# A diffusion transformer layer: weights split into two fp32r parts, kept in DRAM by the first token block

## The chip, the cores and the metric

The kernel runs on one core of a Trainium2 chip. The metric is the device time of one execution in microseconds (us). The core has engines that run side by side, each through its own list of instructions in order: PE (TensorE, matrix products; its weight loads are listed as PEld), DVE (VectorE), ACT (ScalarE), POOL (GpSimd) and SP, which here only issues transfers. ACT and POOL issue transfers too. All transfers run on the core's 16 DMA engines.

## The reference, cut to what matters

The layer works on 2048 latent tokens of width 1024 (four blocks of 512) and 256 context tokens.

```
n = modulate(rmsnorm(x))                                # the context tokens alike
q, k, v, u, gate_attn, gate_ssm = split(n @ w_in)       # 1024 x 4096
att = neighbourhood_attention(rope(q), rope(k), v)      # 8 heads, window 8 x 16 and all context keys
ssm = s5_scans(u); val, gate = split(gelu(ssm) @ w_glu); ssm = val * sigmoid(gate)
mix = (sigmoid(gate_attn) * (att @ w_branch_attn) + sigmoid(gate_ssm) * (ssm @ w_branch_ssm)) @ w_out
h = x + g1 * mix
a, b = split(modulate(rmsnorm(h)) @ w_ffn_in)           # 1024 x 5632
out = rmsnorm(h + g2 * ((silu(a) * b) @ w_ffn_out))
```

## The kernel before, in words

Every product of fp32 matrices is made of three products of fp32r parts (`mm3`, lines 89 to 94): high by high, high by low, low by high. So each weight piece, 128 partitions by 1024 fp32, is loaded (`raw`, line 73), its high part is a copy to fp32r on ACT (line 70) and its low part the difference on DVE (line 71). `piece` (line 79) does the three steps. The raw pieces have two buffers (`wr`; three in the merges, four in the FFN), the parts three each (`wh`; four in the FFN).

`cols` (line 96) gives products with weights at rest: a piece feeds one or two output column groups over the 512 tokens of a block. `rows` (line 111) gives products with tokens at rest: a column of 256 outputs needs two pieces, of four k-tiles each, and both for every 128 tokens.

The stages, in the order of time:

- `norm_u` norms all tokens, keeps them in DRAM (`ns`) and makes u.
- `in_proj` (line 350) goes over the four token blocks, 28 pieces a block: k, v, q, then the gates. Block 0 has the context tokens too. At the start of block 1 stands `biases`, which makes the attention's bias tables on POOL.
- `s5` and `attention` run at the same time as `in_proj`. A scheduler orders every engine's list by its own estimate of times and by priority: s5 and attention go first, and in-projection and merge work fills TensorE between them.
- `merge` (line 939), once per token block, has 20 pieces: GLU (4, w_glu), the branches (4 of w_bs, 4 of w_ba, in turn), output projection (8, w_out). Its first two blocks run beside attention. `modulation2` loads its own weights there, one piece for each piece of the merge (the generator `between`).
- `ffn` (line 1104) goes over the four blocks: `ffn_in` (line 1026) makes sums of its weights on POOL and seven products in place of eight, then the silu and the second product.

Weights are the same in all token blocks, and each block loads and splits them again. Silu is made as tanh(a/2) on ACT and (1 + t) * a on DVE (lines 1133, 1134); the factor 1/2 that is then missing is in the gate `g[1]` (line 228).

SP issues nearly all transfers: raw weights, q and k stores, s5's small strips (`mt`), attention results (`as`), gates (`gsc`), x. POOL issues the loads of s5's inputs (`ut`, line 651), of the bias tables and of attention (`k`, `kc`, `qh`, `ql`, `vt`, `bi`).

Of the kernel before, what the change touches and what calls it, by code (L numbers as in the profile page):

```python
# [10 lines left out]
F32 = mybir.dt.float32  # L11
# [7 lines left out]
P = 128  # L19
# [33 lines left out]
class Kernel:  # L53
# [24 lines left out]

    def piece(self, src, r, c, nr):

        raw = self.raw(src, r, c, nr)
        with self.hot():
            hi = self.wh.tile([P, nr, 1024 // nr], F32R, name="whi")
            lo = self.wh.tile([P, nr, 1024 // nr], F32R, name="wlo")
            self.split(hi, lo, raw)
        next(self.between, None)
        return hi, lo

# [6 lines left out]

    def cols(self, pool, src, kt, c0, n, ops, tag="ps"):

        nm = 8 // kt  # L100
        for c in range(n):
            w = self.piece(src, 0, c0 + c, kt)
            for m in range(nm):
                sl = slice(m * P, (m + 1) * P)
                for i, (nt, f) in enumerate(ops):
                    ps = pool.tile([P, nt], F32, name=tag)
                    for k in range(kt):
                        self.mm3(ps, (w[0][:, k, sl], w[1][:, k, sl]), f(k), k == 0, k == kt - 1)
                    yield c * nm + m, i, ps

    def rows(self, pool, src, c, ops, tag="ps"):


        w = [self.piece(src, r, c, 4) for r in range(2)]
        for i in range(0, len(ops), 2):
            ps = pool.tile([P, 2, 256], F32, name=tag)
            for j in range(2):
                for k in range(KD):
                    self.mm3(ps[:, j], ops[i + j](k), (w[k // 4][0][:, k % 4], w[k // 4][1][:, k % 4]), k == 0, k == KD - 1)
            yield i, ps  # L120
# [6 lines left out]
    def constants(self):  # L127
# [21 lines left out]
        self.us = d.tile([LA, AW], F32, name="us")  # L149
        self.ns = d.tile([NB, KD, P, 2, TB], F32, name="ns")  # L150
        self.gsc = d.tile([2, KD, NB, P, TB], F32, name="gsc")
        self.hs = d.tile([L, D], F32, name="hs")
# [55 lines left out]
    def modulation2(self, tp, pp):  # L208
# [4 lines left out]
        for sec in (2, 3, 4, 5):  # L213
            for c2 in range(2):
# [9 lines left out]
                if sec in (2, 5):  # L224
                    pg = pp.tile([P, 512], F32, name="ps")
                    nc.tensor.matmul(pg, self.ones, acc, start=True, stop=True)
                    with self.hot():
                        V.tensor_scalar(self.g[sec // 5][:, c2 * 512:c2 * 512 + 512], pg, 0.5, None, op0=ALU.mult)
                else:
# [120 lines left out]
    def in_proj(self, ring, ev, pm, nt, nct):  # L350
        nc, I = self.nc, self.I
        V = nc.vector
        for b in range(NB):
            if b:
                nt = [ring.tile([P, 2, TB], F32R, name="n") for _ in range(KD)]
                for k in range(KD):
                    nc.sync.dma_start(nt[k].bitcast(F32), self.ns[b, k])
            t0 = b * TB
            cs = ev.tile([P, 2, TB], F32, name="cs", bufs=1)
            nc.sync.dma_start(cs, I["rope"][:, :, t0:t0 + TB])  # L360
# [9 lines left out]
            def qk(c0, ops, isk):  # L370
                for jj, i, ps in self.cols(pm, I["w_qk"], KD, c0, 4, ops):
                    with self.hot():
# [31 lines left out]
            for c in range(2):  # L404
# [3 lines left out]
                oc = slice(c * 256, c * 256 + 256)  # L408
                for i, ps in self.rows(pm, I["w_vu"], c, ops):
                    e = ev.tile([P, 2, 256], F32, name="e")  # L410
# [11 lines left out]
            for gi in range(2):  # L422
                for m, _, ps in self.cols(pm, I["w_gate"], KD, gi * 8, 8, [lat]):
                    g = ev.tile([P, TB], F32, name="e")
                    with self.hot():
                        nc.scalar.activation(g, ps, AF.Tanh, scale=0.5)
                    nc.scalar.dma_start(self.gsc[gi, m, b], g)
# [511 lines left out]
    def merge(self, b, yp, mp, tp, pm):  # L939
# [5 lines left out]
        op = [(TB, lambda k: (y[k][:, 0], y[k][:, 1]))]  # L945
        ssm = []
        for m2 in range(2):
            tg = []
            for _, _, ps in self.cols(pm, I["w_glu"], 4, 2 + m2, 1, op):
                t = tp.tile([P, TB], F32, name="t")  # L950
                with self.hot():
                    nc.scalar.activation(t, ps, AF.Tanh, scale=0.5)
                tg.append(t)
            for m, _, ps in self.cols(pm, I["w_glu"], 4, m2, 1, op):
                s = yp.tile([P, 2, TB], F32R, name="y")
# [11 lines left out]
        for m2 in range(4):  # L967
            part = {}
            for z, wn, gi in ((ssm, "w_bs", 1), (att, "w_ba", 0)):
                for m, _, ps in self.cols(pm, I[wn], 4, m2, 1, [(TB, lambda k, z=z: (z[k][:, 0], z[k][:, 1]))]):  # L970
                    mm = m2 * 2 + m
# [9 lines left out]
        for c in range(4):  # L981
            cs = slice(c * 256, c * 256 + 256)
            ops = [lambda k, j=j: (mh[:, k, j * P:(j + 1) * P], ml[:, k, j * P:(j + 1) * P]) for j in range(4)]
            for i, ps in self.rows(pm, I["w_out"], c, ops):
                ts = slice(b * TB + i * P, b * TB + (i + 2) * P)
# [40 lines left out]
    def ffn_in(self, ch, b, X, pm, os, tp, up):  # L1026
# [33 lines left out]
        for x in src:  # L1060
            with self.hot():
                hi = self.wh.tile([P, x.shape[1], 4, P], F32R, name="whi")
                lo = self.wh.tile([P, x.shape[1], 4, P], F32R, name="wlo")
                self.split(hi.rearrange("p a k m -> p a (k m)"), lo.rearrange("p a k m -> p a (k m)"), x)
# [39 lines left out]
    def ffn(self, xs_, os, xp, tp, pm, first):  # L1104
        nc, I = self.nc, self.I
        V = nc.vector
        with ExitStack() as ctx:
# [13 lines left out]
            for b in range(NB):  # L1121
# [4 lines left out]
                for g, (p0, p1) in enumerate(groups):  # L1126
                    last = g == len(groups) - 1
                    zs = {}
                    for m2 in range(p0, p1):
                        ts = []  # L1130
                        for a in self.ffn_in(m2, b, X, pm, os, wp, up):
                            t = wp.tile([P, TB], F32, name="n")
                            nc.scalar.activation(t, a, AF.Tanh, scale=0.5)
                            V.scalar_tensor_tensor(t, t, 1.0, a, op0=ALU.add, op1=ALU.mult)
                            ts.append(t)
# [218 lines left out]
```

## Time and profile before

| | |
|---|---|
| median of 3 runs | 3211.07 us (3209.65 to 3219.78) |
| the profiled execution's own time | 3210.19 us |
| its span | 3208.4 us |
| TensorE busy | 3088.2 us, 96% |
| DVE / ACT / POOL busy | 2340.6 / 1567.5 / 899.4 us |
| moved by DMA | 564.27 MB, mean 176 GB/s |

The span goes from the first to the last recorded instruction; the time has 1.8 us around it. Busy times of engines overlap, so they do not add up to the span. PE stands for matrix products that are pipelined: an instruction's own duration is longer than its distance to the next. A wait is the idle time of an engine before an instruction, with what ended it.

### The profile page before, as it was taken

How to read it: one execution, taken by the hardware profiler on the slowest of the kernel's cores; microseconds unless marked ns; L12 is line 12 of the kernel's file. 1: busy time of each engine (PE TensorE's matmuls, PEld its weight loads, DVE VectorE, ACT ScalarE, POOL GpSimd, SP SyncE). 2: the span in 40 equal slices, each digit the busy share in tenths (PEclk: the TensorE clock that was granted, in tenths of full speed). 3: DMA queues.
4: the chain of work that ended last, by engine and by line, in shares of the span. 5: the costliest groups of instructions: out<-in, count | busy, mean ns of one | idle time of the engine just before them, and what ended most of it. 6: DMA issues, size and time to landing. Idle time of an engine off the chain costs nothing.

```text
span 3208.4 us, 54284 instructions
## 1 busy us (share of the span) xinstructions
PE 3088.2 (96%) x20600; PEld 2716.4 (85%) x20600; DVE 2340.6 (73%) x4153; ACT 1567.5 (49%) x2746; POOL 899.4 (28%) x856
## 2 busy tenths in 40 slices
PE   7999978999999899999999999999999999999998
PEld 5988766787788788788888998989989998989988
DVE  6689787897753576665657866987868966886766
ACT  4545434454355556466554543454535543554534
POOL 2000053000223232222300544742242423341243
PEclk9999999999999999999999999999999999999999
DMA  8545467454676898887947434434434433443332
GB/s 320 187 126 170 162 195 239 170 163 143 205 242 186 268 277 241 254 250 223 267 152 248 141 122 139 148 129 134 133 128 150 135 112 125 148 145 128 116 109 102
DMA packets 212852, 564.27 MB, mean 176 GB/s; under 512 B 31784, under 2 KB 63656, under 8 KB 212592
## 3 DMA queue, kind: packets, MB, share of 16 engines
q1 hardware_dynamic: 155008, 437.48, 41.4%
q0 software_dynamic: 28032, 87.64, 10.1%
q10 hardware_dynamic: 29552, 35.70, 3.3%
q8 instruction: 162, 2.65, 0.3%
q14 instruction: 98, 0.80, 0.1%
HBM read 446.95 MB, written 111.61 MB: 174 GB/s over the span
## 4 chain that ended last, share of the span: by engine, by line
PE 74%; DVE 10%; DMA 10%; issue 3%; POOL 2%; ACT 1%; SPq 0%; ACTq 0%; POOLq 0%; DVEq 0%
PE ps L92 14%; PE ps L93 14%; PE ps L94 14%; PE ps L1075 8%; PE ps L1073 7%; PE ps L1074 7%; DVE wlo L71 3%; PE o L924 2%; DMA n<-in_rpb 2%; PE w L905 1%; PE w L884 1%; PE pv L750 1%; DMA y<-as 1%; PE c L886 1%; PE c L907 1%
## 5 line engine op out<-in xcount | busy, mean ns | idle before, releaser
L71 DVE TENSOR_TENSOR wlo<-raw,whi 128x1024 fp32r<-128x1024 f32 (+1 forms) x522 | 681.3, 1312 | 338.1 <-ACT whi L70 336.6
L70 ACT CAST whi<-raw 128x1024 fp32r<-128x1024 f32 (+1 forms) x522 | 508.1, 976 | 493.1 <-PE ps L94 184.7
L1073 PE MATMUL ps<-X,whi 128*128 128x256 f32 x2464 | 693.9, 284 | 14.0 <-DVE u L1085 8.6
L1075 PE MATMUL ps<-X,wlo 128*128 128x256 f32 x2464 | 693.3, 284 | 11.6 <-DVE wlo L71 11.5
L1074 PE MATMUL ps<-X,whi 128*128 128x256 f32 x2464 | 690.7, 283 | 0.0
L1073 PEld LDWEIGHTS ps<-X,whi 128*128 128x128 f32 x2464 | 472.0, 192 | 18.3 <-DVE u L1085 11.3
L1075 PEld LDWEIGHTS ps<-X,wlo 128*128 128x128 f32 x2464 | 471.3, 191 | 15.0 <-DVE wlo L71 14.8
L1074 PEld LDWEIGHTS ps<-X,whi 128*128 128x128 f32 x2464 | 472.0, 192 | 0.5
L92 PE MATMUL ps<-n,whi 128*128 128x512 f32 (+1 forms) x800 | 316.8, 396 | 6.9 <-ACT t L382 5.1
L94 PE MATMUL ps<-n,wlo 128*128 128x512 f32 (+1 forms) x800 | 314.8, 394 | 0.0
L93 PE MATMUL ps<-n,whi 128*128 128x512 f32 (+1 forms) x800 | 314.7, 393 | 0.0
L92 PE MATMUL ps<-whi,zh 128*128 128x512 f32 x704 | 277.1, 395 | 0.0
L94 PE MATMUL ps<-whi,zl 128*128 128x512 f32 x704 | 277.0, 394 | 0.0
L93 PE MATMUL ps<-wlo,zh 128*128 128x512 f32 x704 | 276.9, 394 | 0.0
L1056 POOL TENSOR_TENSOR os<-raw 128x512 f32<-128x512 f32 x66 | 117.4, 1779 | 396.7 <-DMA raw<-in_w_f 326.5
L70 ACT CAST whi<-os 128x1024 fp32r<-128x1024 f32 x110 | 115.4, 1049 | 208.7 <-PE ps L1074 83.9
L71 DVE TENSOR_TENSOR wlo<-os,whi 128x1024 fp32r<-128x1024 f32 x110 | 151.7, 1379 | 67.8 <-ACT whi L70 67.8
L92 PEld LDWEIGHTS ps<-n,whi 128*128 128x128 f32 x800 | 150.5, 188 | 46.0 <-ACT t L382 6.8
L93 PEld LDWEIGHTS ps<-n,whi 128*128 128x128 f32 x800 | 150.5, 188 | 34.6 <-issue 3.4
L1057 POOL TENSOR_TENSOR os<-raw,os 128x512 f32<-128x512 f32 x88 | 134.3, 1526 | 161.6 <-DMA raw<-in_w_f 159.7
L94 PEld LDWEIGHTS ps<-n,wlo 128*128 128x128 f32 x800 | 150.4, 188 | 34.1 <-issue 2.0
L92 PE MATMUL ps<-y,whi 128*128 128x512 f32 x384 | 158.4, 414 | 17.0 <-DMA y<-as 9.7
(343 smaller groups left out, 7025.3 us busy)
## 6 DMA issues: line engine op xcount, KB each, us to landing
raw<-in_w_f SPq DMA_DIRECT2D x198, 512.0 KB
raw<-sums SPq DMA_DIRECT2D x66, 512.0 KB
raw<-in_w_gate SPq DMA_DIRECT2D x64, 512.0 KB
raw<-in_w_f SPq DMA_DIRECT2D x66, 256.0 KB
raw<-in_w_qk SPq DMA_DIRECT2D x32, 512.0 KB
gsc<-e ACTq DMA_DIRECT2D x64, 256.0 KB
raw<-in_w_m SPq DMA_DIRECT2D x32, 512.0 KB
t<-gsc SPq DMA_DIRECT2D x64, 256.0 KB
```

The costliest lines, as they stand in the source:

```text
L70: self.nc.scalar.copy(hi, x)
L71: self.nc.vector.tensor_tensor(lo, x, hi.bitcast(F32), op=ALU.subtract)
L92: mm(ps, l[0], r[0], start=first, stop=False)
L93: mm(ps, l[0], r[1], start=False, stop=False)
L94: mm(ps, l[1], r[0], start=False, stop=last)
L750: nc.tensor.matmul(pv[g2 * 64:g2 * 64 + 64, ri, 0:SEQC], win[:, d, p, g2, ri], rhs, start=True, stop=True, skip_group_check=True)
L924: return nc.tensor.matmul(o[h, g, :, hf, :], l, r, start=(n == 0), stop=(n == nb + 1), skip_group_check=True)
L1056: nc.gpsimd.tensor_tensor(s24[:, 0], s13[:, 0], a11, op=ALU.subtract)
L1057: nc.gpsimd.tensor_tensor(s24[:, 1], a12, s24[:, 0], op=ALU.subtract)
L1073: mm(dst, a[0][:, k], xh, start=(first and k == 0), stop=False, skip_group_check=True)
L1074: mm(dst, a[0][:, k], xl, start=False, stop=False, skip_group_check=True)
L1075: mm(dst, a[1][:, k], xh, start=False, stop=(k == 3), skip_group_check=True)
```

## The change

`piece` now has one tile `w` for both parts. In the first token block it loads and splits as before, then stores both parts, 128 x 2048 fp32, to DRAM: from POOL's queue in `in_proj` (tensors `wk`), from SP's in `merge` (tensors `wm`). In the other three blocks it loads both parts by one transfer straight into `w`, with no raw tile and no split. In the FFN nothing is stored; its parts share one tile too. Silu is one activation on ACT, and the factor of `g[1]` is 1.

```diff
-    def piece(self, src, r, c, nr):
-
-        raw = self.raw(src, r, c, nr)
-        with self.hot():
-            hi = self.wh.tile([P, nr, 1024 // nr], F32R, name="whi")
-            lo = self.wh.tile([P, nr, 1024 // nr], F32R, name="wlo")
-            self.split(hi, lo, raw)
+    def piece(self, src, r, c, nr, kept=None, queue=None):
+
+
+        w = self.wh.tile([P, 2, nr, 1024 // nr], F32R, name="w")
+        flat = w.rearrange("p i k f -> p i (k f)").bitcast(F32)
+        if kept is not None and queue is None:
+            self.nc.sync.dma_start(flat, kept)
+        else:
+            raw = self.raw(src, r, c, nr)
+            with self.hot():
+                self.split(w[:, 0], w[:, 1], raw)
+            if kept is not None:
+                queue.dma_start(kept, flat)
         next(self.between, None)
-        return hi, lo
+        return w[:, 0], w[:, 1]
...
+        self.wk = [d.tile([n, P, 2, 1024], F32, name=f"wk{i}") for i, n in enumerate((8, 4, 16))]
+        self.wm = {w: d.tile([n, P, 2, 1024], F32, name=f"wm_{w}") for w, n in (("w_glu", 4), ("w_bs", 4), ("w_ba", 4), ("w_out", 8))}
...
-                        V.tensor_scalar(self.g[sec // 5][:, c2 * 512:c2 * 512 + 512], pg, 0.5, None, op0=ALU.mult)
+                        V.tensor_scalar(self.g[sec // 5][:, c2 * 512:c2 * 512 + 512], pg, 0.5 if sec == 2 else 1.0, None, op0=ALU.mult)
...
+            fill = None if b else nc.gpsimd
...
-                for jj, i, ps in self.cols(pm, I["w_qk"], KD, c0, 4, ops):
+                for jj, i, ps in self.cols(pm, I["w_qk"], KD, c0, 4, ops, kept=self.wk[0], queue=fill):
...
+        fill = None if b else nc.sync
...
-            for i, ps in self.rows(pm, I["w_out"], c, ops):
+            for i, ps in self.rows(pm, I["w_out"], c, ops, kept=self.wm["w_out"], queue=fill):
...
-                hi = self.wh.tile([P, x.shape[1], 4, P], F32R, name="whi")
-                lo = self.wh.tile([P, x.shape[1], 4, P], F32R, name="wlo")
+                hl = self.wh.tile([P, 2, x.shape[1], 4, P], F32R, name="w")
+                hi, lo = hl[:, 0], hl[:, 1]
...
-                            nc.scalar.activation(t, a, AF.Tanh, scale=0.5)
-                            V.scalar_tensor_tensor(t, t, 1.0, a, op0=ALU.add, op1=ALU.mult)
+                            nc.scalar.activation(t, a, AF.Silu)
```

Since the scheduler orders every list anew, instructions move on all engines. POOL's list before, while block 0 of the in-projection runs, holds the loads of s5's inputs (`ut`) and then the first bias load:

```order
L260 TENSOR_TENSOR r<-ms,mhalf 128x4
L651 DMA ut<-us 128x8x64 x2
L651 DMA ut<-us 32x8x64
L651 DMA ut<-us 128x8x64 x2
L651 DMA ut<-us 32x8x64
L651 DMA ut<-us 128x8x64 x2
L651 DMA ut<-us 32x8x64
L651 DMA ut<-us 128x8x64 x2
L651 DMA ut<-us 32x8x64
L651 DMA ut<-us 128x8x64
```

The same place after:

```order
L660 DMA ut<-us 128x8x64
L91 DMA wk_86<-w 128x2048
L660 DMA ut<-us 128x8x64
L660 DMA ut<-us 32x8x64
L91 DMA wk_87<-w 128x2048
L660 DMA ut<-us 128x8x64 x2
L91 DMA wk_87<-w 128x2048
L660 DMA ut<-us 32x8x64
L660 DMA ut<-us 128x8x64
L91 DMA wk_87<-w 128x2048 x2
L91 DMA wk_86<-w 128x2048 x3
L660 DMA ut<-us 128x8x64
```

The stores of the parts (`wk`) stand between the loads.

SP's list before, at the start of merge 0 (`raw` are weights, `in_w_m` those of `modulation2`, `as` attention results out, `y` the branch inputs in, `t<-gsc` gates in):

```order
L936 DMA as<-a 128x1024
L944 DMA y<-ys 128x2x512 x4
L76 DMA raw<-in_w_m 128x1024
L76 DMA raw<-in_w_bs 128x1024
L76 DMA raw<-in_w_m 128x1024
L76 DMA raw<-in_w_ba 128x1024
L76 DMA raw<-in_w_m 128x1024
L973 DMA t<-gsc 128x512 x4
L76 DMA raw<-in_w_bs 128x1024
L973 DMA t<-gsc 128x512
```

The same place after:

```order
L953 DMA y<-ys 128x2x512 x4
L91 DMA wm_w_glu<-w 128x2048
L76 DMA raw<-in_w_m 128x1024
L76 DMA raw<-in_w_bs 128x1024
L76 DMA raw<-in_w_m 128x1024
L91 DMA wm_w_glu<-w 128x2048
L76 DMA raw<-in_w_ba 128x1024
L91 DMA wm_w_bs<-w 128x2048
L76 DMA raw<-in_w_m 128x1024
L945 DMA as<-a 128x1024
L983 DMA t<-gsc 128x512 x4
L91 DMA wm_w_ba<-w 128x2048
```

Each weight piece's store (`wm`) now stands among the loads, behind its split.

SP's list before, at the output projection of merge 3 (`t<-in_x` is x, `in_w_f` the FFN's first weights, `h` its residual):

```order
L76 DMA raw<-in_w_out 128x1024 x2
L973 DMA t<-gsc 128x512 x3
L76 DMA raw<-in_w_out 128x1024
L973 DMA t<-gsc 128x512 x3
L76 DMA raw<-in_w_out 128x1024
L987 DMA t<-in_x 128x2x256
L76 DMA raw<-in_w_out 128x1024
L987 DMA t<-in_x 128x2x256 x2
L1038 DMA raw<-in_w_f 128x1024 x2
L1160 DMA h<-hs 128x512
L987 DMA t<-in_x 128x2x256 x2
L76 DMA raw<-in_w_out 128x1024
```

The same place after:

```order
L85 DMA w<-wm_w_out 128x2048
L983 DMA t<-gsc 128x512
L997 DMA t<-in_x 128x2x256 x2
L85 DMA w<-wm_w_out 128x2048
L997 DMA t<-in_x 128x2x256
L85 DMA w<-wm_w_out 128x2048
L997 DMA t<-in_x 128x2x256
L1048 DMA raw<-in_w_f 128x1024 x3
L997 DMA t<-in_x 128x2x256
L1169 DMA h<-hs 128x512
L997 DMA t<-in_x 128x2x256
L85 DMA w<-wm_w_out 128x2048
```

Loads of both parts stand where raw loads stood; by the list of TensorE each second piece of an output column there is read after 24 products with the first.

## Rows read from the trace of the kernel before

**Rows 1.** The page's busy time of each engine, share of the span and instructions.

```profile
PE 3088.2 (96%) x20600; PEld 2716.4 (85%) x20600; DVE 2340.6 (73%) x4153; ACT 1567.5 (49%) x2746; POOL 899.4 (28%) x856
```

**Rows 2.** Stretches: length, busy us PE, PEld, DVE, ACT, POOL; clock, DMA share, GB/s.

```profile
0.00:160.00 160.00, 141.44 (x1111) 123.60 (x1112) 104.28 (x372) 78.25 (x124) 24.02 (x24) 0.96 0.69 255
160.00:370.00 210.00, 208.65 (x1270) 172.57 (x1270) 169.00 (x360) 100.81 (x219) 10.59 (x13) 1.00 0.50 152
370.00:560.00 190.00, 159.51 (x848) 126.83 (x847) 159.80 (x279) 78.00 (x164) 67.06 (x68) 0.96 0.67 206
560.00:1020.00 460.00, 454.09 (x2578) 367.01 (x2576) 333.30 (x689) 222.18 (x439) 60.88 (x101) 0.99 0.60 186
1020.00:1410.00 390.00, 366.83 (x2539) 309.81 (x2538) 247.34 (x560) 206.83 (x370) 108.17 (x181) 0.97 0.86 257
1410.00:1730.00 320.00, 313.59 (x2272) 273.55 (x2271) 201.58 (x463) 183.77 (x352) 70.42 (x113) 0.99 0.71 220
1730.00:2164.00 434.00, 415.93 (x2924) 387.49 (x2922) 339.58 (x408) 197.19 (x319) 213.98 (x129) 1.00 0.42 144
2164.00:3208.00 1044.00, 1028.14 (x7071) 955.55 (x7071) 785.74 (x1028) 500.43 (x764) 344.24 (x229) 0.99 0.39 128
```

**Rows 3.** Groups by line: shapes, count, busy us, mean ns, idle before and releasers.

```profile
L71 DVE TENSOR_TENSOR wlo<-raw,whi 128x1024 fp32r<-128x1024 f32 x434 | 585.9, 1350 | 319.2 <-ACT whi L70 317.8
...
L70 ACT CAST whi<-raw 128x1024 fp32r<-128x1024 f32 x434 | 454.6, 1048 | 447.4 <-PE ps L94 163.5 <-PE ps L93 104.3 <-PE ps L1074 92.3
...
L1134 DVE SCALAR_TENSOR_TENSOR n<-n 128x512 f32<-128x512 f32 x88 | 65.5, 779 | 0.2
```

**Rows 4.** The page's rate in 40 equal slices of the span.

```profile
GB/s 320 187 126 170 162 195 239 170 163 143 205 242 186 268 277 241 254 250 223 267 152 248 141 122 139 148 129 134 133 128 150 135 112 125 148 145 128 116 109 102
```

**Rows 5.** Waits of TensorE, 400 to 560 us: total us, times, longest.

```profile
PE pv L750 <- DVE p L758: 8.0, 2, 6.4
...
PE ps L92 <- ACT t L382: 3.7, 3, 2.8
...
PE pv L750 <- ACT win L695: 3.0, 1, 3.0
```

**Rows 6.** Groups by line, 370 to 560 us, the split on DVE.

```profile
L71 DVE TENSOR_TENSOR wlo<-raw,whi 128x1024 fp32r<-128x1024 f32 x22 | 28.0, 1273 | 13.2 <-ACT whi L70 13.1
```

**Rows 7.** Waits of TensorE, whole span.

```profile
PE ps L92 <- ACT whi L70: 8.1, 2, 5.2
```

**Rows 8.** Timeline, a column piece of a merge: start us, us; ten products.

```profile
1717.71 0.40 PE L94 MATMUL ps<-y,wlo 128*128 128x512 f32 x1
...
1719.82 0.39 PE L94 MATMUL ps<-y,wlo 128*128 128x512 f32 x1
```

**Rows 9.** Timeline, an output column of a merge: sixteen products.

```profile
1734.85 0.28 PE L94 MATMUL ps<-whi,ml 128*128 128x256 f32 x1
...
1736.61 0.28 PE L94 MATMUL ps<-whi,ml 128*128 128x256 f32 x1
```

**Rows 10.** Chain of waits: start us, us from issue to landing.

```profile
544.93 6.77 DMA ys<-yt
...
667.65 3.20 DMA raw<-in_w_qk
...
1190.72 8.13 DMA raw<-in_w_out
```

**Rows 11.** Waits of TensorE, 1730 to 2200 us.

```profile
PE ps L1073 <- DVE u L1085: 8.0, 9, 1.6
...
PE ps L1075 <- DVE wlo L71: 7.6, 8, 1.7
```

**Rows 12.** Line 171, the table load: ns minimum, median, maximum.

```profile
L171 ACT ACT_TABLE_LOAD  x1: 1283/1283/1283, 2.1 to 2.1; - x1
```

**Rows 13.** Waits of POOL, whole span.

```profile
POOL ut L651 <- ACT un L652: 389.7, 20, 85.5
```

More of the change, by code (lines that the diff above doesn't have):

```diff
@@ L94, in mm3, with cols @@
         mm(ps, l[1], r[0], start=False, stop=last)
-    def cols(self, pool, src, kt, c0, n, ops, tag="ps"):
+    def cols(self, pool, src, kt, c0, n, ops, tag="ps", kept=None, queue=None):
         nm = 8 // kt
         for c in range(n):
-            w = self.piece(src, 0, c0 + c, kt)
+            w = self.piece(src, 0, c0 + c, kt, kept[c0 + c] if kept is not None else None, queue)
             for m in range(nm):
@@ L109, in cols, with rows @@
                     yield c * nm + m, i, ps
-    def rows(self, pool, src, c, ops, tag="ps"):
-        w = [self.piece(src, r, c, 4) for r in range(2)]
+    def rows(self, pool, src, c, ops, tag="ps", kept=None, queue=None):
+        w = [self.piece(src, r, c, 4, kept[c * 2 + r] if kept is not None else None, queue) for r in range(2)]
         for i in range(0, len(ops), 2):
@@ L408, in in_proj @@
                 oc = slice(c * 256, c * 256 + 256)
-                for i, ps in self.rows(pm, I["w_vu"], c, ops):
+                for i, ps in self.rows(pm, I["w_vu"], c, ops, kept=self.wk[1], queue=fill):
                     e = ev.tile([P, 2, 256], F32, name="e")
@@ L422, in in_proj @@
             for gi in range(2):
-                for m, _, ps in self.cols(pm, I["w_gate"], KD, gi * 8, 8, [lat]):
+                for m, _, ps in self.cols(pm, I["w_gate"], KD, gi * 8, 8, [lat], kept=self.wk[2], queue=fill):
                     g = ev.tile([P, TB], F32, name="e")
@@ L946, in merge @@
         ssm = []
+        fill = None if b else nc.sync
         for m2 in range(2):
             tg = []
-            for _, _, ps in self.cols(pm, I["w_glu"], 4, 2 + m2, 1, op):
+            for _, _, ps in self.cols(pm, I["w_glu"], 4, 2 + m2, 1, op, kept=self.wm["w_glu"], queue=fill):
                 t = tp.tile([P, TB], F32, name="t")
@@ L953, in merge @@
                 tg.append(t)
-            for m, _, ps in self.cols(pm, I["w_glu"], 4, m2, 1, op):
+            for m, _, ps in self.cols(pm, I["w_glu"], 4, m2, 1, op, kept=self.wm["w_glu"], queue=fill):
                 s = yp.tile([P, 2, TB], F32R, name="y")
@@ L969, in merge @@
             for z, wn, gi in ((ssm, "w_bs", 1), (att, "w_ba", 0)):
-                for m, _, ps in self.cols(pm, I[wn], 4, m2, 1, [(TB, lambda k, z=z: (z[k][:, 0], z[k][:, 1]))]):
+                for m, _, ps in self.cols(pm, I[wn], 4, m2, 1, [(TB, lambda k, z=z: (z[k][:, 0], z[k][:, 1]))], kept=self.wm[wn], queue=fill):
                     mm = m2 * 2 + m
```

## The prediction

> **What bounds the kernel now.** I read the page's busy times first, then stretches cut at the stages, then what TensorE waited for in each, then the groups by line, the DMA rows and the chain of waits. TensorE is busy 96% of the span [rows 1], and the clock is granted at 0.96 to 1.00 in every stage [rows 2]. What a change off TensorE can win is therefore its idle time, which the stretches split as follows (length less PE busy) [rows 2]: 18.6 us in the norm and u projection, 1.4 in block 0 of the in-projection, 30.5 in block 1 beside the bias tables, 5.9 in blocks 2 and 3, 23.2 in merges 0 and 1 beside attention, 6.4 in merges 2 and 3, 18.1 in the first FFN block and 15.9 in the other three, 120 us in all. The second thing to see there is the DMA column: 0.86 of the 16 engines' time in merges 0 and 1 at 257 GB/s, against 0.42 in the FFN.
>
> **The change part by part.** It removes the split of 28 pieces in each of three in-projection blocks and of 20 in each of three merges, 144 in all. At 1350 ns on DVE and 1048 on ACT [rows 3] this is 194 us of DVE and 151 us of ACT. Silu on ACT takes the place of Tanh on ACT and of 88 multiplies on DVE at 0.74 us (65.5 us, rows 3). I cost these 410 us at nothing where TensorE runs beside them, and count only TensorE's waits on them.
>
> It adds bytes. A stored piece is 1.05 MB (two parts of 128x1024 fp32), an unsplit one 0.52. Block 0 stores 28 (29.4 MB), merge 0 stores 20 (21.0 MB), and each later block or merge loads 0.52 MB more a piece: 14.7 MB a block, 10.5 a merge. The price of a megabyte has two ends: the first 160 us, mostly SP's transfers over 128 partitions, moved 255 GB/s at a share of 0.69, so 370 GB/s at a full share; merges 0 and 1, mixed with attention's loads, moved 257 at 0.86, so 299 [rows 2]. No slice of the page is above 320 GB/s, and none beside attention above 280 [rows 4].
>
> 1. Block 0, 160 to 370 us. 29.4 MB at 370 GB/s are 79 us of DMA; with 0.50 of 210 us already busy that makes 184 of 210. It fits, but three things have less cover: the store holds its buffer of three until it has landed, SP's raw loads share the engines, and the stores stand on POOL between the s5 loads. Bounds: 0, and the idle share of the stage that runs at 0.86 (23.2 of 390 us), which here gives 12.5 less today's 1.4, +11. I take +6, the middle.
> 2. Block 1, 370 to 560. TensorE's waits are on DVE (8.0 at the s5 products) and ACT (3.7, 3.0) [rows 5]. The splits there are 22 of 1.27 us on DVE [rows 6], 28 of its 160 busy us, and as many of 1.05 on ACT [rows 3], 23 of 78. Bounds: nothing gained, and the whole 14.7 us of the three rows. I take -8, half of them; what is late next is POOL's bias work and the strip transfers, which stay.
> 3. Blocks 2 and 3, 560 to 1020. The one wait is 5.2 us on a split of a v piece [rows 7]; it goes, -5. What is late next is the load in its place. A prepared piece goes straight into one of the three `w` buffers, so it is issued only when TensorE has let go of the piece three before, where before two raw pieces lay ahead as well. For a column piece two pieces of work are left, 48 products 0.234 us apart [rows 8], 11.2 us. For the second piece of a v or output column the order leaves 36 products (the old column's last 12, then 24 on the new column's first piece) at 0.117 us [rows 9], 4.2 us; behind the load in SP's queue stand q, k and x transfers, which nobody waits for at once. A 512 KB load took 3.2 us in a calm place and 8.1 in a busy one, a 1 MB store 6.8 [rows 10]; 512 KB more at 370 GB/s make 4.6 and 9.5 of the loads. Bounds a transition: 0.4 and 5.3 us, I take 2; three v columns, +6. Together +1.
> 4. Merges 0 and 1, 1020 to 1410. 21.0 + 10.5 MB are 85 us of DMA at 370 GB/s and 105 at 299, on top of 0.86 x 390 = 335: 420 or 440 us of work for 390. Behind a full DMA wait, in SP's queue, the loads of the branches, gates and x and the attention results; TensorE runs in order and waits with them. Bounds: 0, if the work spreads into the next stages, and +50. I take +30, the end of SP's own transfers, since the added ones are of that kind. The split wait in this stage (8.1 less the 5.2 of step 3 [rows 7], 2.9) lies inside it and is not counted again.
> 5. Merges 2 and 3, 1410 to 1730. 21 MB are 57 us on 0.71 x 320 = 227, 284 of 320: it fits. The three second pieces of output columns in each merge wait as in 3; 6 x 1.5 us, +9 (bounds 2 and 32).
> 6. FFN. The DVE work that goes is 16.4 us in the first block, of 340 busy. TensorE waits 8.0 and 7.6 us on DVE there [rows 11], in bursts where DVE's queue is behind. Bounds 0 and -18, I take -10, and -5 of the other blocks' 15.9. One tile for both parts frees a buffer one product later (0.12 us), which I leave out. The order has one ACT_TABLE_LOAD more, before the first Silu, 1.28 us [rows 12]: +1.
>
> Sum: 6 - 8 + 1 + 30 + 9 - 15 + 1 = +24 us. On the profiled execution's 3210.2 that is 3234; its time is 0.9 us under the median of the three runs, so 3235.
>
> **A rule weighed.** The stretch of merges 0 and 1 keeps the engines busy 0.86 of the time at 257 GB/s. By the Trainium skill, "DMA: Bandwidth & Descriptors", section "Where 436 GB/s comes from", a core's transfers meet a fabric ceiling of about 435 GB/s and, between HBM and SBUF, about 358. By that the stretch would carry 257 + 31.5 MB in 390 us (81) = 338 GB/s and step 4 would be near nothing. The trace does not agree for this mix: the engines are nearly full there at 257.
>
> **The rivals.** Faster, 3185: relief without collision, in the same stage. The added transfers find room because attention, rid of the splits beside it, issues its loads earlier, in blocks 2 and 3 where the share is 0.60 [rows 2]. Then step 4 is 0 and its split wait of 2.9 us goes as well (-3), step 1 is +1, steps 2, 3 and 6 stay and step 5 is +2: 1 - 8 + 1 - 3 + 2 - 15 + 1 = -21; with the far ends of steps 2 and 3 (-7, -5) it is -33. I take -26. The ceiling in the Trainium skill's DMA page, above, gives the same side. It decides as soon as the stretch stays under a share of about 0.95, so 371 of 390 us, which needs 50 of the 85 us moved elsewhere. For it: 0.60 has 184 us free, of which blocks 2 and 3 take 79 themselves. Against it: three buffers allow no long lead, and merge 0's stores can't come before its splits.
>
> No measurable change, 3211: half of step 4, and the waits on DVE and ACT worth what I took. The cases lie only 50 us apart.
>
> Slower still, 3270: the stores on POOL. POOL waits at the head of its queue for s5's input buffers, 390 us in 20 waits, up to 85.5 [rows 13]; a store behind such a wait keeps its `w` buffer and TensorE stops after two pieces. Against it: the order puts the loads between the stores where they were thought due, and s5 and the in-projection share TensorE, so they can't drift far. With half of the longest wait once, +35 on the forecast.
>
> That the change doesn't do what it says is excluded by the order: DVE has 232 instructions fewer (144 + 88).
>
> **How the numbers follow.** Forecast 0.44 (own range 3221 to 3285), POOL's stores 0.06, no change 0.18, faster 0.32 (3160 to 3201). A measurement of this kernel tells about 0.3%, 10 us, from no change. So slower 0.50, same 0.18, faster 0.32. The range 3175 to 3285 leaves out about a tenth at each end: above it all upper bounds would have to hold, below it nearly all waits on DVE and ACT would have to go with no new one.
>
> **What would show it.** In merges 0 and 1 a DMA share at 0.95 or more, rows of TensorE waiting for loads of `w`, and the stretch longer by some 30 us. In merges 2 and 3 waits of 1 to 3 us on the second piece of an output column, at the first products that read it. In block 0 POOL's stores landing within some 10 us. In the FFN the waits on DVE in the first block halved, and no multiply after Silu. It is wrong if the share in merges 0 and 1 stays under 0.95 with TensorE's idle there at 23 us or less, and its size is wrong if block 0 or block 1 changes by over 12 us.

## The result, and the profile after

The changed kernel takes 3304.1 us (3294.6 to 3306.9), against 3215.4 us for the kernel before, run beside it: ratio 1.0286, 95% interval 1.0263 to 1.031. The forecast of 3235 us had the direction; the loss is 92 us by that ratio, not 24, and outside the range.

The profiled execution has a span of 3301.0 us, 92.6 more than before. First the page's busy times, which answer to [rows 1]:

```profile
PE 3115.8 (94%) x20600; PEld 2741.4 (83%) x20600; DVE 2120.8 (64%) x3921; ACT 1433.4 (43%) x2603; POOL 902.3 (27%) x884
```

DVE lost 220 us and ACT 134, as the change meant, though less than the 260 (194 and 65.5) and 151 that the prediction counted. TensorE has the same 20600 products and yet 27.6 us more of busy time; its idle time rose from 120 to 185 us, and its mean granted clock fell from 0.987 to 0.973. So two thirds of the loss are waits, and one third is products that ran slower. The same stretches of the changed kernel as in [rows 2] (length, busy us of PE, PEld, DVE, ACT, POOL, granted clock, DMA share, GB/s):

```profile
0.00:160.00 160.00, 139.57 (x1070) 120.66 (x1071) 104.08 (x371) 77.36 (x122) 24.09 (x27) 0.94 0.72 271
160.00:370.00 210.00, 208.85 (x1266) 173.63 (x1264) 165.20 (x349) 99.84 (x216) 21.60 (x34) 1.00 0.77 262
370.00:560.00 190.00, 160.94 (x867) 124.17 (x866) 150.47 (x297) 61.82 (x150) 67.01 (x72) 0.93 0.76 248
560.00:1020.00 460.00, 435.52 (x2547) 356.35 (x2546) 266.26 (x653) 181.20 (x404) 75.38 (x125) 0.97 0.77 255
1020.00:1410.00 390.00, 348.46 (x2442) 297.56 (x2442) 183.60 (x477) 191.45 (x345) 110.20 (x182) 0.94 0.90 291
1410.00:1730.00 320.00, 285.32 (x1888) 245.35 (x1888) 161.98 (x390) 121.09 (x255) 59.40 (x90) 0.94 0.83 274
1730.00:2164.00 434.00, 420.46 (x2875) 388.36 (x2874) 260.55 (x304) 154.09 (x269) 154.53 (x94) 0.99 0.53 181
2164.00:3300.00 1136.00, 1116.70 (x7657) 1035.30 (x7655) 828.71 (x1083) 546.50 (x845) 390.05 (x260) 1.00 0.39 130
```

The stretches are the same times in both kernels, but the work in them has moved: the in-projection's last product starts at 1140.9 us where it started at 1055.7, the merges' first at 1152.7 instead of 1066.0, attention's at 858.0 instead of 892.3. Block 0, where 29.4 MB of stores stand, is as full as before (idle 1.2 us). Block 1 did not improve (29.1 against 30.5). Blocks 2 and 3 went from 5.9 to 24.5 us idle, and the two stretches of merges from 29.6 to 76.2, with the clock down from 0.97 and 0.99 to 0.94. What TensorE waited for (total us, times, longest), whole span (before, the second row stood at 4.5 us, the fourth at 8.1, the fifth at 9.7, the sixth at 11.5):

```profile
PE ps L98 <- DMA w<-wk: 24.9, 8, 6.3
PE w L914 <- ACT s L907: 21.8, 9, 5.9
PE ps L98 <- DMA w<-wm_w_out: 19.7, 7, 8.1
PE ps L98 <- ACT w L70: 19.0, 3, 14.0
PE ps L98 <- DMA y<-as: 10.9, 1, 10.9
PE ps L1085 <- DVE w L71: 7.1, 10, 1.2
```

The loads of prepared parts are waited for directly, 44.6 us in the first and third row. The page's row for the column pieces of the in-projection says whom the first row hit: column pieces waited 21.6 of the 24.9 us, the pieces of v the other 3.3.

```profile
L98 PE MATMUL ps<-n,w 128*128 128x512 f32 (+1 forms) x800 | 320.8, 401 | 27.9 <-DMA w<-wk 21.6
```

The second and fourth row lead to transfers too, by ACT, though the second only in part: of its nine waits the longest (5.9 us, to 1226.5) does so for certain. The timeline of ACT shows how:

```profile
1215.39 0.60 ACT L70 CAST mh<-t 128x512 fp32r<-128x512 f32 x1
1223.80 1.04 ACT L70 CAST w<-raw 128x1024 fp32r<-128x1024 f32 x1 [7.81 <-issue]
1224.76 0.87 ACT L905 ACTIVATE s<-s,mn 128x696 f32<-128x696 f32 x1
1225.53 0.19 ACT L905 ACTIVATION_READ_ACCUMULATOR s<-s,mn 128x1 f32 x1
1225.62 0.86 ACT L907 ACTIVATE s<-s,mn 128x696 f32<-128x696 f32 x1
```

ACT stood 7.8 us before the split of a raw piece, which SP had issued at 1211.9 and which by its semaphore events landed at 1223.7; attention's `s`, for which TensorE waited, was queued behind it. Of the fourth row 17.5 us, two waits of 14.0 and 3.5, are splits of merge 0's raw `w_out`, which ACT itself stood waiting for:

```profile
1303.21 1.04 ACT L70 CAST w<-raw 128x1024 fp32r<-128x1024 f32 x1 [14.42 <-DMA raw<-in_w_out]
...
1359.91 1.04 ACT L70 CAST w<-raw 128x1024 fp32r<-128x1024 f32 x1 [4.02 <-DMA raw<-in_w_out]
```

The chain of waits of the changed kernel (start us, us from issue to landing) shows how late they land, against [rows 10]:

```profile
835.43 16.76 DMA w<-wk
...
1275.88 27.31 DMA raw<-in_w_out
```

The first of these loads lost time twice. The piece three before it was last read at 827.4 us, so its buffer was free then, but SP issued the load 8.0 us later: SP's list runs in order, and it stood at a raw load of the merge (`in_w_glu`) that waited for a raw buffer, first for the landing of `in_w_m` and then for DVE. Here are TensorE's last product from that buffer, SP's waits from 826 to 836 us, and SP's timeline:

```profile
827.05 0.39 PE L100 MATMUL ps<-n,w 128*128 128x512 f32 x1
```

```profile
SPq L76 <- DMA raw<-in_w_m: 7.3, 1, 7.3
SPq L76 <- DVE macc L230: 1.6, 1, 1.6
```

```profile
814.68 0.58 SPq L809 DMA_DIRECT2D ys<-yt  x1
...
816.96 0.93 SPq L85 DMA_DIRECT2D w<-wk  x1
...
824.84 0.39 SPq L85 DMA_DIRECT2D w<-wk  x1
825.48 0.55 SPq L809 DMA_DIRECT2D ys<-yt  x1
835.01 0.33 SPq L76 DMA_DIRECT2D raw<-in_w_glu  x1
835.43 25.03 SPq L85 DMA_DIRECT2D w<-wk  x4
```

Then the landing took 16.8 us, with two 1 MB stores of s5 (`ys`), raw loads and two other `wk` loads issued within the 21 us before it. The four longest waits for `wk` (3.0, 4.0, 5.3 and 6.3 us, all at column pieces) are alike when each load is set against its piece: the loads were issued 7.7, 8.6, 3.0 and 8.0 us after their buffer had been released, and landed 15.3, 10.8, 13.4 and 16.8 us after that. During the 8.6 us SP was issuing the rest of sixteen strip transfers (`mt`) and four stores of q, which stood ahead of the load. As an estimate, with the same time to landing and all else unmoved, an issue at the release would have met three of the four waits, all but that of 5.3 us.

What such a wait does to the products behind it is in short stretches around two of them (columns as above):

```profile
825.00:832.65 7.65, 7.65 (x35) 6.12 (x33) 0.46 (x1) 0.60 (x1) 4.94 (x7) 1.00 1.02 348
832.65:838.39 5.74, 0.40 (x3) 0.03 (x1) 1.50 (x2) 0.60 (x1) 0.56 (x1) 0.75 1.02 391
838.39:842.40 4.01, 4.01 (x10) 3.14 (x11) 0.00 (x0) 0.00 (x0) 2.09 (x4) 0.50 1.05 376
842.40:845.67 3.27, 3.27 (x16) 2.61 (x14) 0.00 (x0) 0.00 (x0) 0.83 (x2) 1.00 1.05 262
845.67:852.33 6.66, 0.40 (x3) 0.03 (x1) 0.00 (x0) 0.60 (x1) 0.22 (x1) 0.77 1.02 294
852.33:856.30 3.97, 3.97 (x10) 3.15 (x11) 0.00 (x0) 0.00 (x0) 0.00 (x0) 0.53 1.03 368
```

TensorE stands still for a wait of 5.3 us, then works at 0.50, the lower level of 1.2 GHz, for 4.0 us: ten products where [rows 8] has 17. The wait of 5.3 us costs 7.0. And the DMA engines are full through all six rows, at anything from 262 to 391 GB/s.

### The profile page after: what moved, and what is told of

Its sections match the earlier page's. It is cut to its first block, busy times and chain, and to the rows that moved or that the text cites. A ratio compares the mean times of both kernels' runs of the same rounds, so it can differ in the third digit from the quotient of the medians.

```text
span 3301.0 us, 53943 instructions
## 1 busy us (share of the span) xinstructions
PE 3115.8 (94%) x20600; PEld 2741.4 (83%) x20600; DVE 2120.8 (64%) x3921; ACT 1433.4 (43%) x2603; POOL 902.3 (27%) x884
## 3 DMA queue, kind: packets, MB, share of 16 engines
q0 software_dynamic: 32064, 117.00, 11.2%
## 4 chain that ended last, share of the span: by engine, by line
PE 65%; DMA 11%; DVE 6%; issue 2%; POOL 2%; ACT 1%; SPq 0%; ACTq 0%; DVEq 0%; POOLq 0%
PE ps L98 12%; PE ps L99 11%; PE ps L100 11%; PE ps L1085 8%; PE ps L1083 7%; PE ps L1084 7%; DMA w<-wm_w_out 2%; PE o L933 2%; DMA raw<-in_w_m 2%; DVE w L71 2%; DMA n<-in_rpb 1%; PE w L914 1%; DMA raw<-in_w_out 1%; DMA w<-wk 1%; PE w L893 1%
## 5 line engine op out<-in xcount | busy, mean ns | idle before, releaser
L1083 PE MATMUL ps<-X,w 128*128 128x256 f32 x2464 | 693.6, 283 | 9.7 <-DVE u L1095 5.5
L1084 PE MATMUL ps<-X,w 128*128 128x256 f32 x2464 | 691.8, 282 | 0.0
L1085 PE MATMUL ps<-X,w 128*128 128x256 f32 x2464 | 684.7, 283 | 7.1 <-DVE w L71 7.1
L71 DVE TENSOR_TENSOR w<-raw,w 128x1024 fp32r<-128x1024 f32 (+1 forms) x378 | 499.0, 1328 | 256.0 <-ACT w L70 254.4
L70 ACT CAST w<-raw 128x1024 fp32r<-128x1024 f32 (+1 forms) x378 | 358.6, 949 | 324.2 <-PE ps L100 184.2
L1083 PEld LDWEIGHTS ps<-X,w 128*128 128x128 f32 x2464 | 469.9, 191 | 12.6 <-DVE u L1095 7.0
L1085 PEld LDWEIGHTS ps<-X,w 128*128 128x128 f32 x2464 | 464.4, 191 | 10.2 <-DVE w L71 10.2
L1084 PEld LDWEIGHTS ps<-X,w 128*128 128x128 f32 x2464 | 470.0, 191 | 0.5
L98 PE MATMUL ps<-n,w 128*128 128x512 f32 (+1 forms) x800 | 320.8, 401 | 27.9 <-DMA w<-wk 21.6
L99 PE MATMUL ps<-n,w 128*128 128x512 f32 (+1 forms) x800 | 318.9, 399 | 0.0
L100 PE MATMUL ps<-n,w 128*128 128x512 f32 (+1 forms) x800 | 317.6, 398 | 0.0
L99 PE MATMUL ps<-w,zh 128*128 128x512 f32 x704 | 277.3, 394 | 0.0
L100 PE MATMUL ps<-w,zl 128*128 128x512 f32 x704 | 277.1, 394 | 0.0
L98 PE MATMUL ps<-w,zh 128*128 128x512 f32 x704 | 276.6, 394 | 0.0
L98 PEld LDWEIGHTS ps<-n,w 128*128 128x128 f32 x800 | 153.2, 192 | 69.2 <-issue 28.3
L71 DVE TENSOR_TENSOR w<-os,w 128x1024 fp32r<-128x1024 f32 x110 | 148.3, 1348 | 78.1 <-ACT w L70 78.1
L98 PE MATMUL ps<-w,mh 128*128 128x256 f32 x512 | 150.6, 295 | 37.2 <-DMA w<-wm_w_out 19.7
L100 PEld LDWEIGHTS ps<-n,w 128*128 128x128 f32 x800 | 153.0, 191 | 34.9 <-issue 2.0
L99 PEld LDWEIGHTS ps<-n,w 128*128 128x128 f32 x800 | 153.2, 191 | 34.1 <-issue 3.2
```

The costliest lines, as they stand in the source:

```text
L70: self.nc.scalar.copy(hi, x)
L71: self.nc.vector.tensor_tensor(lo, x, hi.bitcast(F32), op=ALU.subtract)
L98: mm(ps, l[0], r[0], start=first, stop=False)
L99: mm(ps, l[0], r[1], start=False, stop=False)
L100: mm(ps, l[1], r[0], start=False, stop=last)
L1083: mm(dst, a[0][:, k], xh, start=(first and k == 0), stop=False, skip_group_check=True)
```

## Experiments

Theories. *Late loads*: a prepared piece is issued only when the third buffer comes free, where raw pieces lay two further ahead; TensorE waits for the landing. *Bytes*: 126 MB more fill the engines, wherever the loads stand. *Order*: the scheduler's new lists cost by themselves. In the table "over Silu" is the ratio less that of Silu alone, times 3210 us; a ratio's interval is 0.0012 to 0.0031 to each side, so with Silu's own a difference "over Silu" is uncertain by some 6 to 11 us.

| what the kernel has | ratio to before (95%) | over Silu, us |
|---|---|---|
| Silu alone | 0.9969 (0.9953 to 0.9985) | 0 |
| all, as changed | 1.0286 (1.0263 to 1.0310) | +102 |
| in_proj's parts | 1.0052 (1.0032 to 1.0071) | +27 |
| in_proj's parts, four places | 0.9974 (0.9962 to 0.9986) | +2 |
| merges' parts | 1.0134 (1.0109 to 1.0160) | +53 |
| merges' parts, four places in 2 and 3 | 1.0136 (1.0118 to 1.0155) | +54 |
| all, four places (merges: 2 and 3) | 1.0103 (1.0080 to 1.0126) | +43 |
| all, loads of half the size | 1.0130 (1.0099 to 1.0161) | +52 |
| all stores, raw loads and splits | 1.0031 (1.0019 to 1.0043) | +20 |
| the same, and the low parts stored again | 1.0126 (1.0104 to 1.0149) | +50 |
| all, merge 0's stores from POOL | 1.0253 (1.0236 to 1.0270) | +91 |
| block 0's stores alone | 1.0045 (1.0029 to 1.0060) | +24 |
| merge 0's stores alone | 1.0054 (1.0035 to 1.0074) | +27 |
| the same, an eighth of the bytes | 1.0020 (1.0008 to 1.0032) | +16 |
| merges, loads of half the size | 1.0084 (1.0059 to 1.0109) | +37 |
| merges, raw loads, low parts stored again | 1.0084 (1.0058 to 1.0111) | +37 |
| merges 2 and 3 alone (and merge 0's stores) | 1.0086 (1.0062 to 1.0111) | +38 |
| FFN's second weights alone | 0.9960 (0.9946 to 0.9974) | -3 |
| FFN's, and in_proj's with four places | 0.9984 (0.9970 to 0.9999) | +5 |

**Parts of the change.** Silu alone (the diff's last lines on the kernel before); in_proj without the merges, and the reverse (`kept=..., queue=fill` taken out of the other calls).

> The kernel before with Silu alone (one activation on ACT, factor of g[1] 1). In the changed kernel the stretch from the first FFN product to the end went from 1431 to 1424 us, 8 us less. Late loads (TensorE waits for pieces whose load is issued too late), bytes (the added transfers fill the DMA engines) and order (the scheduler's new lists) all expect that gain alone here: 3207 us, within 3200 to 3215. Above 3220 would say that Silu itself costs.

> The changed kernel with the merges as before (raw loads and splits); only in_proj stores and loads parts. Late loads: the waits for wk (24.9 us) and the slower products behind them stay, about +50 -8: 3255. Bytes: 73 MB of the added 126 in stages whose DMA engines had room, +20 -8: 3227. Order: the in-projection's end at 1141 instead of 1056 us comes from the lists, nearly all stays: 3290.

> The changed kernel with in_proj as before; only the merges store and load parts. Late loads: the waits for wm (22 us) and the slower products behind them, +40 -8: 3245. Bytes: the 52 MB fall where the DMA engines were at 0.86, +60 -8: 3265. Order: attention starts where it did, little is left: 3210.

3201, 3225 and 3252 us. Silu keeps its gain. in_proj came out at the figure of bytes and 30 under that of late loads, the merges between the two; order, with 3290 and 3210, missed both. The merges cost twice what in_proj does, and the two together (+80) are less than the change (+102). In the merges' kernel the stretch 1020 to 1410 reached the share that the prediction named as its sign:

```profile
1020.00:1410.00 390.00, 352.64 (x2458) 296.87 (x2458) 217.20 (x531) 196.98 (x358) 112.66 (x186) 0.96 0.98 309
```

**Bytes against lead, all stages.** Loads of half the size:

```diff
-            self.nc.sync.dma_start(flat, kept)
+            self.nc.sync.dma_start(flat[:, 0], kept[:, 0])
+            next(self.between, None)
+            return w[:, 0], w[:, 0]
```

> The changed kernel, but the later token blocks load only the high part (0.52 MB as a raw piece) and use it for the low part too, so two of the three products have wrong weights. Issue points and buffers as changed, bytes of the loads as before, stores stay (50 MB). Late loads: they land sooner, but are still issued at the third buffer's release; half of the added waits stay: 3260. Bytes: only the stores are left, 3230. Order: 3300 as the changed kernel.

Stores alone (later blocks take the `raw` way), and then with `self.nc.sync.dma_start(kept[:, 1], flat[:, 1])` behind each later split:

> The changed kernel, but the later token blocks load raw weights and split them as before; block 0 and merge 0 still store both parts (50 MB), which nobody reads. It prices the stores. With Silu alone the time was 3201. My prediction's terms for the stores (6 in block 0, and of the 30 in merges 0 and 1 the 21 of 31.5 MB, 20): 3227. Late loads: stores only hold a buffer, 3210. Bytes: half of what the change costs over Silu alone, as half-size loads left: 3250.

> As the kernel with stores alone, and each piece of the later token blocks stores its low part too (0.52 MB, SP's queue), so the bytes of every stage are those of the changed kernel (126 MB more than before) while raw loads, their buffers and the splits are as before. Bytes: as slow as the changed kernel, 3290. Late loads: the raw loads keep their lead of two raw buffers, so no more than 15 over stores alone: 3235.

3250, 3220 and 3251 us. The kernel of half loads and that of stores alone move the same 614.6 MB (the page's DMA line), and differ by 32 us: the price of the place of the loads at half size, net of the splits saved. The changed kernel and that of all bytes move 690.1 MB and differ by 51: the same price at full size. The second halves (in the kernel of all bytes stores in place of loads) cost 30 where raw loads keep their lead, and 50 where the loads stand at the third buffer. Neither theory alone has it; the two prices are of one size, and each comes out some 20 higher where the other is paid, which is no more than new lists may be worth (see the stores below). The 20 us of the stores are not bytes alone, as the kernel with an eighth of them shows below.

**A fourth place**, in the raw buffers that idle once nothing is split:

```diff
...
+            self.nk += 1
+            if self.deep and self.nk % 4 == 0:
+                w = [self.wr.tile([P, nr, 1024 // nr], F32, name="raw") for _ in range(2)]
+                for i in range(2):
+                    self.nc.sync.dma_start(w[i].rearrange("p k f -> p (k f)"), kept[:, i])
...
```

> The changed kernel, but every fourth prepared piece of in_proj's later blocks and of merges 2 and 3 goes into the two idle raw buffers (two loads of 0.52 MB), so that four pieces lie in buffers in place of three; bytes as changed. Late loads: the waits for wk (25 us) and half of those for wm_w_out (10 of 20) go with the slower products behind them, 40 off: 3260. Bytes: a buffer more doesn't make transfers faster where the engines are full, 10 off at most: 3290.

> in_proj alone stores and loads parts, with the fourth place in the idle raw buffers; merges as before, Silu on. Without the fourth place it took 3225, Silu alone 3201. Late loads: the 23.6 us of waits for wk and the slower products behind them go, the stores and the 44 MB of second halves are left at some 10: 3205. Bytes: at most 8 of the 24 come back, 3217.

> The merges alone store and load parts, with the fourth place in merges 2 and 3; in_proj as before, Silu on. Without the fourth place 3252. Late loads: the waits for wm_w_out (20.0 us, five) are in merges 1 to 3, two thirds go with the slower products behind them, 20 off: 3232. Bytes: the cost is in merges 0 and 1, which keep three places, 3248.

3243, 3201 and 3253 us. In in_proj the bytes are the same, and the cost is gone, with the waits for the loads. The stretch 560 to 1020 and the wait for `wk` from 560 us on, first with three places, then with four:

```profile
560.00:1020.00 460.00, 435.04 (x2559) 355.91 (x2558) 265.24 (x650) 181.26 (x404) 75.28 (x125) 0.97 0.77 255
```

```profile
PE ps L98 <- DMA w<-wk: 22.4, 5, 6.9
```

```profile
560.00:1020.00 460.00, 456.07 (x2743) 373.71 (x2741) 273.39 (x684) 194.56 (x431) 87.01 (x145) 0.99 0.82 271
```

```profile
PE ps L107 <- DMA w<-wk: 3.0, 1, 3.0
```

The DMA share is higher with four places (0.82 against 0.77), and TensorE idles 3.9 us where it idled 25.0. The lists are new here too (attention starts at 815 us instead of 858), but nearly all of the 21 us of idle time that went are waits for `wk`. A further place covers both losses of the load, the stand in SP's list and the long landing; how much each counts was not tried apart. In the merges it gave nothing: the stretch 1410 to 1730 idles 23.9 us in place of 25.9, and that of merges 0 and 1, which keep three places, 40.2 in place of 37.4. A new wait stands at the FFN's first weights (TensorE's waits of that kernel, 1800 to 1840 us), where the merges with three places have 0.5; that the fourth place holds the raw buffers which these weights need is likely, not shown:

```profile
PE ps L1092 <- ACT w L71: 9.9, 1, 9.9
```

**Stores.** Merge 0's from POOL; block 0's alone; merge 0's alone; merge 0's with `kept[0:16]`, `flat[0:16]`:

> The changed kernel with merge 0's stores in POOL's queue in place of SP's; nothing else. If the loads of x, gates, attention results and raw weights were held by standing behind the stores in SP's queue, 20 off: 3280. If the engines are simply full there (bytes), or the cost is in the later loads: 3300.

> Silu, and block 0 of in_proj stores its parts from POOL's queue (29 MB, never read); the rest as before. My prediction's term 1 says +6 over Silu alone: 3207. If the 20 us of all stores go by bytes, 12 of them are here: 3213. If the stores cost only in merge 0, where the engines were at 0.86: 3201.

> Silu on, in_proj as before, merge 0 stores both parts (21 MB) from SP's queue, nobody reads them; merges 1 to 3 load raw weights and split them. Lead alone, bytes alone and merges 2 and 3 alone each gave 3235, and these stores are what the three have in common. If the stores carry the merges' cost: 3230. If each of the three has a cost of its own, as bytes and late loads expect: 3208.

> Merge 0's stores alone, as before this run, but each store writes only 16 of the 128 partitions (2.6 MB in all in place of 21): the same 20 instructions at the same splits, an eighth of the bytes. If the 27 us of these stores are bytes: 3204. If they are the place of the stores (they stand in SP's queue until the split is done and the loads behind them wait; the buffer is held until they land): 3222.

3292, 3224, 3228 and 3218 us. The queue matters little (11 us, about the uncertainty). By the Trainium skill, "DMA: Bandwidth & Descriptors", section "Issuing engines are not separate DMA queues", transfers of all issuing engines end on the same 16 engines and interleave there; the run, with its 11 us, agrees. Block 0's stores do nothing to their own stage (TensorE busy 209.1 of 210 us), but two waits stand later, in attention and in block 1, which Silu alone has at 0.4 us and not at all:

```profile
PE w L891 <- ACT pl L920: 17.2, 3, 9.5
PE ps L96 <- ACT e L419: 12.1, 1, 12.1
```

Those products wait for ACT's copies, and ACT stood before them at loads: at an input of s5 that POOL had issued behind its bias work (the wait of 12.1), and at raw weights of the merges (waits of 9.5 and 5.4).

```profile
468.94 0.62 ACT L659 COPY un<-ut 128x512 f32<-128x512 f32 x1 [15.94 <-DMA ut<-us]
...
1214.81 1.04 ACT L70 CAST w<-raw 128x1024 fp32r<-128x1024 f32 x1 [11.22 <-DMA raw<-in_w_out]
...
1372.14 1.04 ACT L70 CAST w<-raw 128x1024 fp32r<-128x1024 f32 x1 [8.22 <-DMA raw<-in_w_bs]
```

The last store of block 0 was issued at 384 us, and behind it this kernel has the bytes of Silu alone: what differs there is the lists and the times. Both stores together cost less (20) than either alone (24, 27), 31 us under their sum. So new lists by themselves may be worth some 25 to 30 us between these kernels. None of them tries the lists alone, so this stays open, and a difference of that size counts here only where rows of a trace carry it. Merge 0's stores are surer: the FFN-weights kernel below has the same starts of attention (875 us) and of the merges' first products (within 4 us) and idles 28 us in the stretch 1020 to 1410, this one 45, the eighth 31. First the kernel of the FFN's weights, then merge 0's stores, then an eighth of them:

```profile
1020.00:1410.00 390.00, 361.65 (x2490) 307.73 (x2491) 240.72 (x538) 203.44 (x359) 107.45 (x179) 0.96 0.86 254
```

```profile
1020.00:1410.00 390.00, 345.26 (x2343) 290.93 (x2343) 221.15 (x516) 196.84 (x350) 111.55 (x185) 0.93 0.93 290
```

```profile
1020.00:1410.00 390.00, 358.65 (x2438) 304.47 (x2438) 237.62 (x526) 198.27 (x347) 100.02 (x165) 0.96 0.86 257
```

With an eighth of the bytes share and idle fall back nearly to the first row, while the time keeps 16 of the 27 us: within the intervals the bytes are worth some 11, and the rest isn't seen in this stretch.

**The merges' cost**, bytes against lead, and by merge:

> The merges alone (Silu on, in_proj as before), and merges 1 to 3 load only the high part (0.52 MB, used for the low part too, so two of three products there are wrong). Bytes of loads as before, 21 MB of stores more, three places. Full loads took 3252, Silu alone 3201. Late loads: most of the 51 stays, 3240. Bytes: the share in merges 0 and 1 falls back from 0.98, 3210.

> The counterpart: Silu on, in_proj as before; merge 0 stores both parts, merges 1 to 3 load raw weights and split them as before, and store the low part (0.52 MB) once more, so that the bytes are those of full loads (52 MB more than before) and the raw loads keep their buffers. Bytes: 3245. Late loads: 3212.

> The merges alone, with merge 1 as before (raw loads and splits); merge 0 stores, merges 2 and 3 load parts. If the 51 us come from merge 1 and its attention (share 0.98 up to 1410 us, two of the waits for wm_w_out, 13 of 20 us): 3212. If merges 2 and 3 carry two thirds of it, by their second pieces or by attention, which goes on beside merge 2: 3235.

All three gave 3235 us: nearer to late loads in the first, to bytes in the second, and the figure of merges 2 and 3 in the third. They share merge 0's stores (27). What each adds to these is 10 us, within the uncertainty, and the full change of the merges adds 26. So the stores' kernel holds half of the merges' cost, with the doubt about lists that stands above, and of the other half neither bytes nor lead is shown to be the whole.

**The same scheme where transfers have room**, `piece` with `self.wf[...]` in the FFN's second product, and with in_proj's four places:

> The same scheme elsewhere: Silu, and only the FFN's second weights (22 pieces) are stored in the first token block and loaded by the others (four places there); in_proj and merges as before. The FFN's DMA share is 0.35 to 0.42 and it waits 10 us for splits of the first weights, none for these. Late loads and bytes both expect no cost there: 3201, within 3194 to 3206.

> The two parts that cost nothing by themselves with Silu: in_proj stores and loads parts with four places, and the FFN's second weights are stored and loaded; merges as before. 3200.9 and 3197.2 apart. If their small reliefs add up, 3195; if only Silu gains and the rest is even, 3200.

3197 and 3204 us. It costs nothing there and gains nothing that can be told from Silu alone. These kernels, like all in the table but the first, have one tile for both parts, so that tile is not what costs in the others. Silu alone and the kernel of the FFN's second weights both beat the kernel before and the changed one; between them the intervals don't decide.

## Why the prediction was wrong, step by step

The sign, step 4's mechanism and the sign of silu held; step 3 failed, and a price was missing. Forecast and result are 68 us apart. By the table 28 of these are in_proj (steps 1 to 3 say -1, measured +27), 14 the merges (39 and 53), 4 Silu (-14 and -10), and 22 come only with in_proj and merges together.

- Step 3, "Together +1": this is what failed. It charged a late load only at the second piece of a v column, +6 (for three columns, where blocks 2 and 3 have four), and took the 11.2 us before a column piece as ample, since loads were to land within 4.6 to 9.5 us of the buffer's release [rows 10]. Measured in the changed kernel, v pieces waited 3.3 us in all and column pieces 21.6. SP issued the loads of the four longest waits 3.0 to 8.6 us after the release, and they then landed after 10.8 to 16.8. The step looked at what stands behind the load in SP's queue, not at what stands ahead of it. in_proj's parts cost 27 us in all, and with a fourth place 2; so it was the lead, at the pieces that the step took as covered. The long end of the landing decides, and I used a typical one.
- The missing price: the same products took 27.6 us longer. Each term priced a wait at its own length. Two waits with the slow products behind them stand above; that all of the 27.6 come this way is not shown one by one. The Trainium skill has the rule that I left out, "TensorE: Matmul & The Clock Gate", section "HAM oscillation — how this bites in real kernels": where TensorE stands for data again and again, the clock's fall is paid behind each wait. The short stretches above agree (0.50 and 0.53 granted after waits of 5.3 and 6.3 us).
- Step 4, +30: DMA full, as said (share 0.98 at 309 GB/s with the merges alone, 0.90 in the changed kernel, where the merges start later); raw loads of merge 0 landed after up to 27.3 us. But merges cost 53 against 39 with step 5's +9 in it, and one way of it was not in the sum: ACT stands in order at a split whose raw piece is late. TensorE waited 17.5 us for two such splits of merge 0's `w_out`, and 5.9 us for an `s` of attention queued behind another. Also my stretches put attention beside merges 0 and 1 alone. In the kernel before its last product starts at 1670.6 us, and merge 3's first products start at 1652 us, so attention lies beside all of merge 2, and step 5's "it fits" was reckoned too kindly; loads of `w_out` were waited for up to 8.1 us, and up to 10.1 with the merges alone, beyond the bound of 5.3.
- Step 1, +6: none in its stage, +24 for these stores alone elsewhere in the span, at ACT's waits for other loads; whether the new lists or the stores caused them, the runs don't settle. The POOL rival fell: POOL's stores landed in 7.9 us at the median, and block 0 idled 1.2 us.
- The faster rival: its condition came in part. Attention started at 858 us instead of 892, and blocks 2 and 3 carried a share of 0.77 instead of 0.60, but TensorE waited there for the prepared parts.
- Step 2, -8: nothing came. The waits of [rows 5] shrank (the first from 8.0 to 1.8 us from 400 to 560), but waits for `n<-ns` (5.2 us), `wk` (3.0) and s5's `h` (8.4) stood in their place; "what is late next" was named, and not charged.
- Step 6, -15 + 1: Silu alone gave -10 (5 to 15). TensorE's waits on splits and `u` in the FFN stayed in part. The right size.
- The rule weighed: 309 GB/s at a share of 0.98 is under the 338 that the stretch would have needed. The section "Where 436 GB/s comes from" of the Trainium skill's "DMA: Bandwidth & Descriptors" has some 358 between HBM and SBUF; this mix does not reach it over 390 us, though the short stretches above show 376 and 391.
- The terms do not add: in_proj +27 and merges +53, together +102; why the two together cost 22 more stays open. What the runs show of it is that in_proj with four places took 27 - 2 = 25 back, and all with four places 59.

## What to carry to other kernels

Keeping a prepared operand in DRAM trades engine work that may be hidden for bytes, and it removes a stage of buffers: count how many pieces lie ahead after the change, and set that against the longest landing in the busiest stretch, not the median, and against what the load has to stand behind in its own queue. When a stage is freed, give its buffers to the loads, and see who needs them next. Where the bound engine is 96% busy, relief of the others is worth only the waits on them: here 134 us of ACT and 220 of DVE, Silu's part included, bought no more than Silu's 10 us that these runs can show.

## What was not expected of the hardware

- After a wait of 5.3 us TensorE's clock was granted at 0.50 for 4.0 us, after 6.3 us at 0.53 for 4.0. The products of the changed kernel took 27.6 us longer, likely for it and waits like it, though the mean clock fell only from 0.987 to 0.973.
- Full DMA engines (share 1.02 to 1.05) moved 262 to 391 GB/s in stretches of 3 to 8 us next to each other; over whole stages the rate divided by the share goes from 299 (before, 1020 to 1410) to 376 (after, 0 to 160). The rate at a full share goes with the mix of transfers here, so a megabyte has no one price.
